# Gated conv + state-space trunk in float32: a new buffer layout, another load queue and fixed priorities in the combination stage

## The chip, the cores and the metric

The kernel runs on one core of one Trainium2 chip. The metric is the device time of one execution in microseconds (us); the median of three executions is given, with the lowest and the highest. Differences under about 0.3% of it can't be told from noise here.

A core has a matrix engine (PE, with its weight loads PEld), a vector engine (DVE), an activation engine (ACT) and GpSimd (POOL). SyncE (SP) only issues transfers. DVE, ACT, POOL and PE each work through their own instructions strictly in the order laid down when the kernel is built.

## The reference

One decoder layer over 1024 positions and 1024 channels, all float32:

```python
h = layer_norm(x, ln_in_g, ln_in_b)
u = h @ w_in                      # -> conv GLU, z, x/B/C, dt, gate_a, gate_b
v = a * sigmoid(g);  v = causal_dwconv(v, 31 taps)
y_a = silu(layer_norm(v)) @ w_conv_out
y   = ssd_chunked(x * dt, ...)    # state-space scan, 32 heads, 4 groups, chunks of 128
y_b = (rms_norm_per_group(y * silu(z)) * norm_w) @ w_ssm_out
mix = (sigmoid(gate_a) * y_a + sigmoid(gate_b) * y_b) @ w_o
h = layer_norm(alpha * h + mix)
h = layer_norm(alpha * h + conv_ffn(h))
```

The change touches how `y_a`'s layer norm, `y_b`'s group norm and the two gated sums are scheduled. What is computed stays the same.

## The kernel before

**Tiling.** Positions are worked in two halves of 512 (`hh` 0 and 1). Channels lie on the 128 partitions, positions along the free axis. Every float32 product is made of three products of rounded parts (`mm3`, lines 170 to 172): a *column* of 128 output channels over 1024 inputs is 24 matmuls of 128x512 (`project`), and it fills one of four PSUM banks (`bank(1)`, tile `acc`). A column's weights are loaded by SP (line 145), rounded on ACT (line 147), and their remainder made on DVE (line 151).

**Order.** A planner lays out each engine's instructions at build time: it runs a model of the machine and gives each engine the ready instruction that stands first. Where an instruction stands is its place in the program; `tc.high_priority(offset=n)` puts it n places earlier, with a negative n later. The places inside such a block don't count for what follows. On the chip every engine then keeps to that order, whatever is ready.

**Mixers** (`mixers`, one call for each half). For each of four groups: two columns for B and C, four for X, four for z, four for the conv GLU; then `ssd_group`, four chunks of 128 positions. A chunk is a chain over PE (transposes 497 to 501, products 536, 539, 544), ACT (504, 511, 514) and DVE (531, 554, 562, 565, 566). While a group's chunks run, PE fills its time with the next group's columns. `conv4` takes an X column out of its bank (ACT 404, 406) into a tile of `x4`, which has two slots: group g+1 writes where group g-1 was.

After its four chunks a group is normalised: `scaled` sums squares over partitions by a product with ones (PE 573), then square root (ACT 581), reciprocal (DVE 582), a trip through DRAM to spread the row over partitions (POOL 584, 585), and four multiplications (DVE 588). `parts` then makes rounded part (ACT 601) and remainder (DVE 602) of the group; only then is its `x4` slot free. For group g, both stand in the program right ahead of `ssd_group` of group g+1. `conv31` is the 31-tap convolution: 60 DVE steps for each group's pair of tiles (line 453), set 1500 places back so that DVE does them when it has nothing else. The first six of its eight tiles are stored to DRAM (463); the last two stay in memory.

**Combination** (`combine`). Eight gate columns (`gate`, sigmoid on ACT 669) alternate with eight columns of the second half of the state-space output; each is added to a stored partial sum `yb` (SP 677) and multiplied by its gate (DVE 681, 682) into `mb0` to `mb7`. Then come the layer norm of the eight convolved tiles: six are loaded back (SP 692), POOL adds all eight (697, 699), PE averages over partitions (701, the *mean product*), DVE subtracts, ACT squares, POOL adds up (710), PE averages again (712), and the tiles are scaled, passed through silu and split into `sT`. This norm stands after the eight columns in the program and is set 900 places ahead. Eight columns over `sT` follow. In the first half the input norm of the second half is made at the end (`ln_in_second`).

**Memory.** The pool of `combine` lies on the bytes of the pool of `mixers`, tile by tile in the order in which tags are first used, and each tile waits on the chip for the users of the bytes beneath it alone. Before, the order is gate, yb, mb0 to mb7, the convolved pairs c0 to c2, stats, sq, sT, c3. So the gate tiles lie on `rstd` and `m` of the mixers, yb on `cbm` and `u`, the convolved pairs on `x4`, `stats` and `sq` on `zs`, `c3` on the last tiles, `rows` and `ya`.

Of the kernel before, what the change touches and what calls it, by code (L numbers as in the profile page):

```python
# [8 lines left out]
F32 = mybir.dt.float32  # L9
# [7 lines left out]
P = 128  # L17
# [38 lines left out]
def kernel(  # L56
# [212 lines left out]
    def ln_in_second(pl):  # L269
# [14 lines left out]
        return hT  # L284
# [188 lines left out]
    def ssd_group(pl, hh, g, xT, BT, CT, zs):  # L473
# [10 lines left out]
        for c in range(4):  # L484
# [81 lines left out]
            V.tensor_add(ssum[:, cs], sq[:, 0], sq[:, 1])  # L566

        def scaled():
            rstd = pl.tile([P, HALF], F32, tag="rstd", name=f"rstd{hh}_{g}")
            rows = pl.tile([P, P], F32, tag="rows", name=f"rows{hh}_{g}")  # L570
            pv = bank(0)
            for j in range(4):
                TE.matmul(
                    pv[j * HEADS : (j + 1) * HEADS, :P],
                    ones[:, :HEADS],
                    ssum[:, j * P : (j + 1) * P],
                    start=True,
                    stop=True,
                    tile_position=(0, j * HEADS),
                )  # L580
# [16 lines left out]
        def parts(yT):  # L597
            ks = slice((g % 2) * 4, (g % 2) * 4 + 4)
            hi, lo = yT[:, 0, ks], yT[:, 1, ks]
            for n in (slice(0, 2), slice(2, 4)):  # L600
                A.copy(hi[:, n], xT[:, n])
                V.tensor_tensor(
                    out=lo[:, n], in0=xT[:, n], in1=hi[:, n].bitcast(F32), op=ALU.subtract
                )

# [19 lines left out]
    def mixers(hh, hT):  # L625
        pre = first_columns(hh, hT, (CT_B, CT_C, CT_X))
        with pool(f"mixers{hh}") as pl:
            time_steps(pl, hh, pre[0])
            scaled = parts = None
            for g in range(GROUPS):  # L630
# [12 lines left out]
                if g in (1, 2):  # L643
                    parts(yT)
                split_2 = parts
                scaled, parts = ssd_group(pl, hh, g, xT, BT, CT, zs)
                if g == 3:
                    ssm_out_first(pl, hh, yT)
                    yT = big_tile(f"yT{hh}_2")
                    split_2(yT)  # L650
                    gate_first(pl, hh, hT, range(3))
                    scaled()
                    parts(yT)
# [5 lines left out]
    def combine(hh, hT, yT, accs):  # L659

        with pool(f"comb{hh}") as pl:
            mb, gbs = [], []

            def gate():
                j = len(gbs)
                pg = bank(1)
                project(pg, weights(wcol[CT_GB + j], f"gb{hh}_{j}"), hT)
                gb = pl.tile([P, HALF], F32, tag="gate", bufs=3, name=f"gb{hh}_{j}")
                A.activation(out=gb, in_=pg, func=AF.Sigmoid)
                gbs.append(gb)  # L670

            gate()
            for j in range(8):
                if j < 7:
                    gate()
                ya = pl.tile([P, HALF], F32, tag="yb", bufs=2, name=f"yb{hh}_{j}")
                SY.dma_start(ya, y_scr[hh][j])
                ps = bank(1)
                project(ps, weights(wssm[j, 1], f"sp{hh}_{j}"), yT)
                m = pl.tile([P, HALF], F32, tag=f"mb{j}", name=f"mb{hh}_{j}")  # L680
                V.tensor_add(m, ya, ps)
                V.tensor_mul(m, m, gbs[j])
                mb.append(m)
            with tc.high_priority(offset=900):
                cs = []
                for i in range(8):
                    if i in accs:
                        cs.append(accs[i])
                        continue
                    if i % 2 == 0:  # L690
                        pair = pl.tile([P, 2, HALF], F32, tag=f"c{i // 2}", name=f"cc{hh}_{i}")
                    SY.dma_start(pair[:, i % 2, :], c_scr[hh][i])
                    cs.append(pair[:, i % 2, :])
                stats = pl.tile([P, 2, HALF], F32, tag="stats", name=f"stats{hh}")
                squares = pl.tile([P, 2, HALF], F32, tag="sq", name=f"csq{hh}")
                mean = stats[:, 0, :]
                G.tensor_add(mean, cs[0], cs[1])
                for c in cs[2:]:
                    G.tensor_add(mean, mean, c)
                pm = bank(0)  # L700
                TE.matmul(pm, mean_w, mean, start=True, stop=True)
                var = stats[:, 1, :]
                for i, c in enumerate(cs):
                    V.tensor_tensor(out=c, in0=c, in1=pm, op=ALU.subtract)
                    if i == 0:
                        A.activation(out=var, in_=c, func=AF.Square)
                    else:
                        sq = squares[:, i % 2, :]
                        A.activation(out=sq, in_=c, func=AF.Square)
                        G.tensor_add(var, var, sq)  # L710
                pv = bank(0)
# [4 lines left out]
                for i, c in enumerate(cs):  # L716
# [8 lines left out]
                    split_to(sT, i, c)  # L725
            mixT = big_tile(f"mixT{hh}")
# [8 lines left out]
            return mixT, None if hh else ln_in_second(pl)  # L735
# [554 lines left out]
```

## Time and profile before

| | us |
|---|---|
| median of 3 executions (lowest, highest) | 1969.62 (1964.88, 1970.72) |
| the profiled execution, its own time | 1972.21 |
| its span, first to last instruction | 1970.1 |
| busy: DVE | 1600.7 (81%) |
| busy: ACT | 1083.8 (55%) |
| busy: POOL | 203.1 (10%) |

The profiled execution is 2.1 us longer than its span and 2.6 us above the median. PE's busy time is a union of overlapping matmuls, each shown with its full latency of 0.39 us although the next one starts 0.23 us after it; so a full PE is seen by the number of matmuls in a stretch, and a wait by its gap. The first half's mixers run to about 484 us and its combination to about 626 us; the second half's mixers run from about 660 to 1135 us and its combination to about 1267 us. The rest is the feed-forward part.

### The profile page before, as it was taken

How to read it: one execution, taken by the hardware profiler on the slowest of the kernel's cores; microseconds unless marked ns; L12 is line 12 of the kernel's file. 1: busy time of each engine (PE TensorE's matmuls, PEld its weight loads, DVE VectorE, ACT ScalarE, POOL GpSimd, SP SyncE). 2: the span in 40 equal slices, each digit the busy share in tenths (PEclk: the TensorE clock that was granted, in tenths of full speed). 3: DMA queues.
4: the chain of work that ended last, by engine and by line, in shares of the span. 5: the costliest groups of instructions: out<-in, count | busy, mean ns of one | idle time of the engine just before them, and what ended most of it. 6: DMA issues, size and time to landing. Idle time of an engine off the chain costs nothing.

```text
span 1970.1 us, 25840 instructions
## 1 busy us (share of the span) xinstructions
PE 1932.9 (98%) x9453; PEld 1575.2 (80%) x9453; DVE 1600.7 (81%) x2224; ACT 1083.8 (55%) x1617; POOL 203.1 (10%) x246
## 2 busy tenths in 40 slices
PE   9999999999899999999999999999999999999997
PEld 8888777777688788888778888888888888878886
DVE  7599999999786547898999655587788888879778
ACT  4676767653263265868775435365555555544432
POOL 0001010110310000110101040001000000121010
PEclk9999999999999999999999999999999999999999
DMA  7645455546455665555554644576455555588673
GB/s 270 221 171 198 161 206 177 166 162 202 157 187 176 215 221 182 190 184 198 178 178 148 213 162 129 169 255 227 160 166 183 175 185 184 179 293 297 201 230 125
DMA packets 128416, 378.36 MB, mean 192 GB/s; under 512 B 15104, under 2 KB 15648, under 8 KB 128288
## 3 DMA queue, kind: packets, MB, share of 16 engines
q1 hardware_dynamic: 109152, 321.63, 48.7%
q0 software_dynamic: 12800, 43.54, 6.4%
q10 hardware_dynamic: 6336, 11.54, 1.6%
q8 instruction: 74, 1.21, 0.3%
q14 instruction: 54, 0.44, 0.1%
HBM read 289.99 MB, written 86.65 MB: 191 GB/s over the span
## 4 chain that ended last, share of the span: by engine, by line
PE 71%; DVE 16%; issue 5%; DMA 5%; ACT 2%; POOL 1%; SPq 0%; DVEq 0%; ACTq 0%; POOLq 0%
PE acc L172 16%; PE acc L171 16%; PE acc L170 16%; PE sm L171 6%; PE sm L172 6%; PE sm L170 6%; DVE c L453 5%; DVE w_c L151 1%; DVE x L408 1%; DMA rstd<-nrm_scr 1%; PE sm L536 1%; DMA dr<-wdown 1%; PE sm L539 1%; DVE x L588 1%; DMA b_scr<-fo 1%
## 5 line engine op out<-in xcount | busy, mean ns | idle before, releaser
L170 PE MATMUL acc<-hT,w_c 128*128 128x512 f32 x1000 | 391.8, 392 | 0.5 <-ACT x L406 0.5
L171 PE MATMUL acc<-hT,w_c 128*128 128x512 f32 x1000 | 390.7, 391 | 0.0
L172 PE MATMUL acc<-hT,w_c 128*128 128x512 f32 x1000 | 390.1, 391 | 0.6 <-DVE w_c L151 0.5
L453 DVE SCALAR_TENSOR_TENSOR c<-v,pc,c 128x512 f32<-128x512 f32 x480 | 370.6, 798 | 7.3 <-ACT c L442 4.7
L170 PEld LDWEIGHTS acc<-hT,w_c 128*128 128x128 f32 x1000 | 187.8, 188 | 41.7 <-issue 1.9
L172 PEld LDWEIGHTS acc<-hT,w_c 128*128 128x128 f32 x1000 | 187.8, 188 | 41.2 <-DVE w_c L151 1.4
L171 PEld LDWEIGHTS acc<-hT,w_c 128*128 128x128 f32 x1000 | 187.8, 188 | 39.2 <-issue 1.1
L147 ACT CAST w_c<-st_c 128x1024 fp32r<-128x1024 f32 x128 | 133.8, 1045 | 108.5 <-PE acc L172 90.0
L515 POOL TENSOR_TENSOR ce<-ce,xbc 128x1024 f32<-128x1024 f32 x28 | 74.1, 2648 | 694.3 <-ACT ce L514 694.3
L1077 ACT CAST w_dn<-dr 128x1024 fp32r<-128x1024 f32 (+1 forms) x73 | 68.8, 944 | 87.5 <-DMA dr<-wdown 25.3
L504 ACT ACTIVATE m<-ab,acs 128x128 f32<-128x128 f32 x256 | 78.4, 390 | 48.2 <-PE sm L536 47.0
L170 PE MATMUL sm<-h1s,w_s 128*128 128x512 f32 x264 | 102.7, 389 | 0.0
L171 PE MATMUL sm<-h1s,w_s 128*128 128x512 f32 x264 | 102.7, 389 | 0.0
L172 PE MATMUL sm<-h1s,w_s 128*128 128x512 f32 x264 | 102.2, 389 | 0.0
L151 DVE TENSOR_TENSOR w_c<-st_c,w_c 128x1024 fp32r<-128x1024 f32 x64 | 79.1, 1239 | 22.3 <-ACT w_c L147 22.1
L1078 DVE TENSOR_TENSOR w_dn<-dr,w_dn 128x1024 fp32r<-128x1024 f32 (+1 forms) x73 | 78.7, 1089 | 5.3 <-ACT w_dn L1077 5.3
L408 DVE SCALAR_TENSOR_TENSOR x<-u,pc,x 128x512 f32<-128x512 f32 x96 | 76.7, 810 | 5.7 <-ACT x L406 5.7
L172 PE MATMUL acc<-h1b,w_ue 128*128 128x512 f32 x176 | 68.9, 395 | 1.5 <-DVE w_ue L151 1.5
L170 PE MATMUL acc<-h1b,w_ue 128*128 128x512 f32 x176 | 68.8, 391 | 0.0
L171 PE MATMUL acc<-h1b,w_ue 128*128 128x512 f32 x176 | 68.6, 390 | 0.0
L170 PE MATMUL sm<-h1b,w_s 128*128 128x512 f32 x176 | 68.5, 389 | 0.0
L171 PE MATMUL sm<-h1b,w_s 128*128 128x512 f32 x176 | 68.5, 389 | 0.0
(324 smaller groups left out, 4542.3 us busy)
## 6 DMA issues: line engine op xcount, KB each, us to landing
st_c<-wcol SPq DMA_DIRECT2D x128, 512.0 KB, 4.4
low_scr<-w_c SPq DMA_DIRECT2D x64, 512.0 KB, 2.9
w_c<-low_scr SPq DMA_DIRECT2D x64, 512.0 KB, 4.4
ab<-acs_scr SPq DMA_DIRECT2D x32, 512.0 KB, 4.1
dr<-wdown SPq DMA_DIRECT2D x55, 256.0 KB, 4.8
st_wo<-wo SPq DMA_DIRECT2D x24, 512.0 KB, 4.0
st_ue<-wup SPq DMA_DIRECT2D x22, 512.0 KB, 4.2
first_scr<-first ACTq DMA_DIRECT2D x44, 256.0 KB, 2.9
```

The lines of the kernel that those rows point to most:

```text
L147: A.copy(w[:, 0, :], st)
L151: V.tensor_tensor(out=w[:, 1, :], in0=st, in1=w[:, 0, :].bitcast(F32), op=ALU.subtract)
L170: TE.matmul(ps, wa(0), xa(0), start=start, stop=False, skip_group_check=more)
L171: TE.matmul(ps, wa(0), xa(1), start=False, stop=False, skip_group_check=more)
L172: TE.matmul(ps, wa(1), xa(0), start=False, stop=stop, skip_group_check=more)
L408: V.scalar_tensor_tensor(out=o, in0=u[:, k : k + HALF], scalar=pc[:, wc + k : wc + k + 1], in1=o, op0=ALU.mult, op1=ALU.add,)
L453: V.scalar_tensor_tensor(out=accs[i], in0=v[:, k : k + HALF], scalar=pc[:, wc + k : wc + k + 1], in1=accs[i], op0=ALU.mult, op1=ALU.add,)
L504: A.activation(out=m[:, h, :], in_=ab[:, h, :], func=AF.Relu, scale=-1.0, bias=acs[:, c, 8 * g + h : 8 * g + h + 1],)
L515: G.tensor_tensor(out=ce, in0=ce, in1=CT[:, cs].unsqueeze(1).to_broadcast([P, 8, P]), op=ALU.mult)
L536: TE.matmul(o, xs[:, h * HP : (h + 1) * HP], m[:, h, :], start=True, stop=first)
L1077: A.copy(w[:, 0, cs], src)
L1078: V.tensor_tensor(out=w[:, 1, cs], in0=src, in1=w[:, 0, cs].bitcast(F32), op=ALU.subtract)
```

## The change

`combine` gets its tiles in another order: sq, stats, gate, yb, mb0 to mb7, in the first half c3 (as `x1_3`, for `ln_in_second`), c0 to c2, sT. The norm is cut into three functions. `early_tiles` runs after the first `yb` load: it makes the tiles, loads the six stored convolved tiles from POOL's queue instead of SP's, 5000 places ahead, and adds up the eight tiles on POOL. `deviations` (mean product, differences, squares) stands after pass j = 2 of the loop in the first half and j = 1 in the second; `normed` (second product, scaling, `sT`) after j = 4 and j = 3. The block set 900 places ahead is gone.

In the mixers, the four products with ones of groups 0 to 2 (line 573) are set 300 places back, and the two pieces of `parts` of groups 0 and 1 move from ahead of the next group's chunks to behind its chunks 0 and 1.

```diff
-            xt = pl.tile([P, D], F32, tag=f"c{t}", name=f"x1_{t}")
+            xt = x3 if t == 3 else pl.tile([P, D], F32, tag=f"c{t}", name=f"x1_{t}")
...
             V.tensor_add(ssum[:, cs], sq[:, 0], sq[:, 1])
+            if c < len(between):
+                between[c]()
...
-            pv = bank(0)
-            for j in range(4):
-                TE.matmul(
+            with tc.high_priority(offset=-300 if g < 3 else 0):
+                pv = bank(0)
+                for j in range(4):
+                    TE.matmul(
...
+            return [lambda: part(slice(0, 2)), lambda: part(slice(2, 4))]
...
-                if g in (1, 2):
-                    parts(yT)
+                between = parts(yT) if g in (1, 2) else []
                 split_2 = parts
-                scaled, parts = ssd_group(pl, hh, g, xT, BT, CT, zs)
+                scaled, parts = ssd_group(pl, hh, g, xT, BT, CT, zs, between)
...
+            gbs = []
+            squares = pl.tile([P, 2, HALF], F32, tag="sq", name=f"csq{hh}")
+            stats = pl.tile([P, 2, HALF], F32, tag="stats", name=f"stats{hh}")
+            late, cs = [], []
+            mean, var = stats[:, 0, :], stats[:, 1, :]
+
+            def early_tiles():
+                mb = [pl.tile([P, HALF], F32, tag=f"mb{j}", name=f"mb{hh}_{j}") for j in range(8)]
+                late.extend(
+                    pl.tile([P, D], F32, tag="c3", name=f"x1_{t}") for t in (3,) if not hh
+                )
+                pairs = [
+                    pl.tile([P, 2, HALF], F32, tag=f"c{i}", name=f"cc{hh}_{i}") for i in range(3)
+                ]
+                with tc.high_priority(offset=5000):
+                    for i in range(6):
+                        G.dma_start(pairs[i // 2][:, i % 2, :], c_scr[hh][i])
+                        cs.append(pairs[i // 2][:, i % 2, :])
+                cs.extend(accs[i] for i in (6, 7))
                 G.tensor_add(mean, cs[0], cs[1])
                 for c in cs[2:]:
                     G.tensor_add(mean, mean, c)
+                return mb
...
+            gate()
+            mb = None
+            for j in range(8):
+                if j < 7:
+                    gate()
+                ya = pl.tile([P, HALF], F32, tag="yb", bufs=2, name=f"yb{hh}_{j}")
+                SY.dma_start(ya, y_scr[hh][j])
+                if mb is None:
+                    mb = early_tiles()
+                ps = bank(1)
+                project(ps, weights(wssm[j, 1], f"sp{hh}_{j}"), yT)
+                V.tensor_add(mb[j], ya, ps)
+                V.tensor_mul(mb[j], mb[j], gbs[j])
+                if j == 2 - hh:
+                    deviations()
+                if j == 4 - hh:
+                    sT = normed()
```

More of the change, by code (lines that the diff above doesn't have):

```diff
@@ L471, in z_gate, with ssd_group @@
         return zs
-    def ssd_group(pl, hh, g, xT, BT, CT, zs):
+    def ssd_group(pl, hh, g, xT, BT, CT, zs, between):
         S = states[g]
@@ L599, in parts, with part @@
             hi, lo = yT[:, 0, ks], yT[:, 1, ks]
-            for n in (slice(0, 2), slice(2, 4)):
+            def part(n):
                 A.copy(hi[:, n], xT[:, n])
@@ L649, in mixers @@
                     yT = big_tile(f"yT{hh}_2")
-                    split_2(yT)
+                    for part in split_2(yT):
+                        part()
                     gate_first(pl, hh, hT, range(3))
                     scaled()
-                    parts(yT)
+                    for part in parts(yT):
+                        part()
                 with tc.high_priority(offset=-1500):
@@ L661, in combine @@
         with pool(f"comb{hh}") as pl:
[L662 to L696, printed above, removed]
+            gbs = []
@@ L734, in combine @@
                 split_to(mixT, j, mb[j])
-            return mixT, None if hh else ln_in_second(pl)
+            return mixT, None if hh else ln_in_second(pl, late[0])
     def out_proj(pl, rs, hh, mixT):
```

27 lines of the change are left out of this document (18 added, 9 removed).

## The prediction

> **What bounds the kernel now.** First the page, for the engine that sets the end.
>
> ```profile
> span 1970.1 us, 25840 instructions
> PE 1932.9 (98%) x9453; PEld 1575.2 (80%) x9453; DVE 1600.7 (81%) x2224; ACT 1083.8 (55%) x1617; POOL 203.1 (10%) x246
> ```
>
> PE is filled nearly throughout, and the change adds and removes no product. So it can only give or take time in which PE stands still. Those gaps are named, with their causes, in the view of waits on PE (total us, times, longest):
>
> ```profile
> PE sm L536 <- DVE m L531: 6.5, 5, 1.5
> PE sm L701 <- POOL stats L699: 5.2, 1, 5.2
> ...
> PE sm L573 <- DVE ssum L566: 1.8, 2, 0.9
> ...
> PE acc L170 <- ACT gb L669: 1.6, 1, 1.6
> ...
> PE acc L170 <- ACT x L406: 0.5, 1, 0.5
> ```
>
> Three of these the change works on: the mean product (701), the products with ones (573), the first sigmoids (669). The largest group, 536 waiting for the vector engine, it doesn't name. The stretch table gives the price of the longest wait, by the count of matmuls that began or ran in 20 us:
>
> ```profile
> 500.00:520.00 20.00, 18.37 (x81) 14.91 (x80) 12.43 (x16) 5.69 (x7) 2.91 (x3) 1.00 0.53 180
> 520.00:540.00 20.00, 14.78 (x50) 11.01 (x50) 16.52 (x18) 5.73 (x9) 13.07 (x9) 0.83 0.37 124
> 540.00:560.00 20.00, 20.00 (x88) 16.20 (x87) 14.02 (x14) 11.91 (x15) 6.03 (x5) 1.00 0.35 118
> 1140.00:1160.00 20.00, 20.00 (x88) 16.19 (x88) 9.15 (x11) 6.44 (x9) 10.25 (x7) 1.00 0.61 209
> ```
>
> A full stretch holds 88, so a matmul takes 20/88 = 0.227 us and a column of 24 takes 5.45. From 520 to 540 there are 38 fewer: 8.6 us, of which the wait is 5.2 and the rest the granted clock of 0.83 that follows it (the mean product's own two passes cost some 0.4 more than two plain matmuls). I put **8.2 us** on the mean product's wait. The last row is the second half's combination: full, nothing to win.
>
> **Why the mean product waits.** Timelines of DVE, SP, POOL, PE and ACT:
>
> ```profile
> 506.80 1.57 ACT L669 ACTIVATE gb<-acc 128x512 f32<-128x512 f32 x3
> 511.15 1.53 DVE L453 SCALAR_TENSOR_TENSOR c<-v,pc,c 128x512 f32<-128x512 f32 x2
> 511.63 2.98 SPq L692 DMA_DIRECT2D cc<-c_scr  x6
> 520.75 1.41 DVE L681 TENSOR_TENSOR mb<-yb,acc 128x512 f32<-128x512 f32 x2 [8.07 <-DMA yb<-y_scr]
> 516.76 1.28 POOL L697 TENSOR_TENSOR stats<-cc 128x512 f32<-128x512 f32 x1 [22.01 <-DMA cc<-c_scr]
> 518.29 5.71 POOL L699 TENSOR_TENSOR stats<-stats,cc 128x512 f32<-128x512 f32 x4 [0.25 <-DMA cc<-c_scr]
> 524.08 3.79 POOL L699 TENSOR_TENSOR stats<-stats,c 128x512 f32<-128x512 f32 x2
> 522.32 0.39 PE L172 MATMUL acc<-yT,w_sp 128*128 128x512 f32 x1
> 527.92 2.08 PE L701 MATMUL sm<-stats,mean_w 128*128 128x512 f32 x2 [5.22 <-POOL stats L699]
> ```
>
> The six stored tiles are asked for only at 511.6; five additions follow, then the two tiles kept in memory, which the convolution finished at 511.15 + 1.53 = 512.7. POOL has stood idle for 22 us before. With the six loaded early, on a queue with nothing else to do, only the last two additions follow 512.7.
>
> **The change, part by part.**
>
> *Loads on POOL.* Six issues leave SP (2.98 us), which also sends the yb loads 3 us sooner, and go to POOL, which is 10% busy; the bytes beneath (zs) were last read by the fourth group's chunks, ahead of all the columns from which `combine` starts. Cost on the path: none. Queued behind them on POOL are the group norm's trip through DRAM (584, 585), if the planner puts them first, and the additions; the trip would then wait for the stores of the third group's convolved tiles. I take nothing for it, since POOL was idle for 22 us after that trip.
>
> The Trainium skill ("DMA: Bandwidth & Descriptors", Latency and other measured facts) gives about 1 us to the first byte from GpSimd against 0.6 us from SP: an estimate by that page is 6 x 0.4 = 2.4 us against the change if the loads were late. No row here shows the first byte; the cover of tens of us hides it either way.
>
> *Additions on POOL, earlier.* They now lie beside the convolution, and there the two engines disturb each other:
>
> ```profile
> 428.83 1.40 DVE L453 SCALAR_TENSOR_TENSOR c<-v,pc,c 128x512 f32<-128x512 f32 x2
> 431.66 2.83 POOL L515 TENSOR_TENSOR ce<-ce,xbc 128x1024 f32<-128x1024 f32 x1 [12.29 <-ACT ce L514]
> 432.15 3.54 DVE L453 SCALAR_TENSOR_TENSOR c<-v,pc,c 128x512 f32<-128x512 f32 x2
> ```
>
> Two convolution steps take 1.40 alone and 3.54 beside 2.83 us of POOL: 0.76 us lost for each us of POOL. Five additions of 1.28 cost DVE 4.9 us. The early yb loads put three passes of 681 and 682 (0.7 each step by the row of 520.75, 1.4 a pass) ahead of the convolution, 4.2 us. So the last two tiles come at 512.7 + 4.9 + 4.2 = 521.8, less the idle time of DVE that is filled (bounded by 0 and the 9 us); with two additions, 2.6, the sum is ready between 515 and 524.
>
> *The fixed place.* Behind pass 2, PE has six matmuls more to do than at 522.3, less the 1.8 and 1.6 us of waits that go before it: it arrives at about 520.5 to 522. Against "ready" that leaves a wait of 0 to 4 us; I take **0.5**, as the filled idle time (8.07 us ahead of the first 681 alone) is nearer to all of the loss than to none. Saved: 8.2 - 0.5. Its second product (712) comes four columns, 21.8 us, later; the chain between them is eight differences and squares and seven additions at the 1.43 to 1.9 us of the rows above (5.71/4, 3.79/2), 10 to 13 us, so it stays hidden; without that cover, what exceeds 21.8 us would be PE's wait.
>
> *Sigmoids.* Gate tiles move off `rstd`, which the mixers give up last, onto `u` and `xbc`. The three sigmoids at 506.80 stand in a row, the first for a column that was done long before; banks then run out and PE waits 1.6 us. Whether the planner then puts them earlier, the trace can't say: 0 to 1.6, I take **0.8**.
>
> *Products with ones, 300 places back.* Both waits go: **1.8**. But what hangs behind them comes later too. Counted in the code, 300 places from there are what is left of `scaled` (8), four chunks and parts (about 200) and three columns of about 32: B, C and the first X of the next group. PE, at 98%, nearly always has something ready, so the products slip by some 20 us, and with them the release of the `x4` slot for which the X columns wait:
>
> ```profile
> L573 PE MATMUL sm<-ssum,ones x64: 272/285/297, 192.1 to 1107.5; 128*32 128x128 f32 x64
> ...
> 195.16 0.37 ACT L581 ACTIVATE rows<-sm,eps 128x128 f32<-128x128 f32 x1
> 198.28 0.95 DVE L582 RECIPROCAL rows<-rows 128x128 f32<-128x128 f32 x1
> 199.53 0.61 POOL L584 DMA_DIRECT2D nrm_scr<-rows  x1 [18.31 <-DVE rows L582]
> 203.53 0.58 POOL L585 DMA_DIRECT2D rstd<-nrm_scr  x1 [3.39 <-DMA nrm_scr<-rows]
> 209.37 2.74 DVE L588 SCALAR_TENSOR_TENSOR x<-x,pc,rstd 128x512 f32<-128x512 f32 x4 [3.98 <-DMA rstd<-nrm_scr]
> 212.14 1.05 ACT L601 CAST yT<-x 128x1024 fp32r<-128x1024 f32 x1 [0.27 <-DVE x L588]
> 219.50 2.35 DVE L602 TENSOR_TENSOR yT<-x,yT 128x1024 fp32r<-128x1024 f32 x2
> 222.00 1.27 ACT L406 ACTIVATE x<-acc,pc 128x512 f32<-128x512 f32 x2
> ...
> 228.37 0.44 PE L536 MATMUL sm<-m,xs 128*64 128x128 f32 x4
> ...
> 231.91 0.48 PE L171 MATMUL acc<-hT,w_c 128*128 128x512 f32 x1
> ```
>
> From the product at 192.1 to the X column's exit at 222.0 are 29.9 us. When the products come behind X0, the three other X columns (16.3) and a chunk's products (231.91 - 228.37 = 3.5) can still run, until the four banks are full: 19.9 us of cover. The same stretch stands four times, groups 0 and 1 of both halves. Without the waits between its pieces the chain takes 3.1 (to 195.16) + 0.37 + 0.95 + 4.0 + 5.84 + 2.74 + 1.05 + 2.35 + 0.69 = 21.1, which is 1.2 over the cover; with them 29.9, 10 over. Four times: 4.8 to 40 us. Below, 0, if the planner finds a hole in PE for the products earlier. I take the low end, **4.8**: DVE waits here are queueing behind convolution steps, and with the trip through DRAM (3.98 us of idle DVE), 588 and 602 gone from the stretch before, DVE should have caught up by the time they come. This choice decides most, and is the weakest.
>
> *Between the chunks.* `parts` behind chunks 0 and 1 lets chunk instructions go first; its own steps are the same. What PE waits for the chain, DVE uses: of the 6.5 us at 536 I take **2.4** off (half of 4.8).
>
> **Sum**: -8.2 + 0.5 - 0.8 - 1.8 + 4.8 - 2.4 = **-7.9 us**. Against the profiled execution's 1972.2 (span 1970.1 and 2.1 around it) that is 1964.3; against the median of 1969.6, 2.6 lower, **1961.7**. With the terms at their good ends (0 for the slot, 1.6 for the sigmoids) it is 1957, at their bad ones (4 us for the mean product) 1965.
>
> **Rivals.** *The slot costs what the other terms give.* With half of the queueing left, the chain is about 4 us over the cover in each place: 16, with 5 off at 536: -8.2 + 0.5 - 0.8 - 1.8 + 16 - 5 = +0.7, **1970**. For it: the first X column leaves its bank at 222.00, right as 602 ends (219.50 + 2.35), and at 968.32 the row below names 602 as what it waited for. Against: the one wait of PE named for it (406) is 0.5 us.
>
> *Slower: the slot's chain keeps its length.* The chain, from square root to exit, took much the same everywhere:
>
> ```profile
> 288.49 0.37 ACT L581 ACTIVATE rows<-sm,eps 128x128 f32<-128x128 f32 x1
> 314.63 1.27 ACT L406 ACTIVATE x<-acc,pc 128x512 f32<-128x512 f32 x2
> ...
> 849.05 0.37 ACT L581 ACTIVATE rows<-sm,eps 128x128 f32<-128x128 f32 x1
> 871.83 0.69 ACT L406 ACTIVATE x<-acc,pc 128x512 f32<-128x512 f32 x1
> ...
> 939.80 0.37 ACT L581 ACTIVATE rows<-sm,eps 128x128 f32<-128x128 f32 x1
> 968.32 0.69 ACT L406 ACTIVATE x<-acc,pc 128x512 f32<-128x512 f32 x1 [1.04 <-DVE yT L602]
> ```
>
> That is 26.8, 26.1, 22.8 and 28.5 us, plus 3 ahead: 9 over the cover, 36 in all. With all 6.5 at 536 won back: -10.3 + 36 - 6.5 = +19, **1989**. It decides from (5.9 + 10.3 + 6.5)/4 = 5.7 us over the cover. For it: order is fixed, and a step waits for its place even if its data is there. Against: PE's own waits in those places give DVE time to catch up, so the later chains shorten.
>
> *The change doesn't remove the wait.* DVE hands over the last two tiles late (POOL's additions, 681 and 682 ahead), PE waits some 5 us and loses the clock again: -7.9 + 5 = -2.9, **1967**. The Trainium skill ("GPSIMD Engine Reference", Key points) says that GpSimd shares its memory interfaces with the vector engine and contends with its instructions of two inputs in SBUF. The 3.54 against 1.40 us above agrees; by it the convolution, with two such inputs, always pays.
>
> **How the numbers follow.** About 0.3%, 5.9 us, is what a measurement tells from no change. Forecast (a gain of 6 to 14): 0.47. Slot gives back the gain: 0.24. Wait stays: 0.07. Slot's full chain: 0.22. So faster 0.47, same 0.31, slower 0.22. The range reaches from 1951 (all 6.5 at 536 gone too) to 1979, about half of the slow case.
>
> **What would show it.** Right: no wait at 701, 88 matmuls and clock 1.00 in every stretch of the first combination; POOL's loads and five additions done well before the convolution ends; 573 behind the first X column, and no column waiting on 406. Wrong: PE waiting for ACT 406 in the groups' second third, four times; 536 waiting longer; or 701 still idle for POOL. If 573 doesn't move, the slot's terms fall away.

## The result and the profile after

| | before | after |
|---|---|---|
| median of 4 executions (us) | 1967.38 | 1997.23 |
| lowest, highest | 1964.88, 1970.72 | 1995.01, 1998.48 |
| ratio, 95% interval | | 1.0149 (1.0128 to 1.0171) |
| the profiled execution (us) | 1972.21 | 1995.01 |
| its span (us) | 1970.1 | 1993.3 |

The change makes the kernel slower by 1.5%, 29.9 us between the medians and 23.2 us between the two profiled spans. The forecast was 1961.7 with a range up to 1979. The first lines of the page after:

```profile
span 1993.3 us, 25854 instructions
...
PE 1944.1 (98%) x9453; PEld 1580.7 (79%) x9453; DVE 1598.4 (80%) x2224; ACT 1085.7 (54%) x1617; POOL 210.8 (11%) x258
```

PE has as many instructions as before and is as "busy"; this line doesn't show where 23 us went. The view of PE's waits after does; its first line (total us, times, longest):

```profile
PE acc L170 <- ACT x L406: 26.8, 4, 10.5
```

The four causes shown of before (536, the mean product, 573, the sigmoids) are all gone from this list. In their place stands one that was 0.5 us: PE waits four times for ACT line 406, which takes X columns out of their banks. The stage borders tell the rest. These rows give, for the kernel before, the first start of the gate columns (the combination begins), of the output product (it ends), and of the second half's gate columns:

```profile
L170 PE MATMUL acc<-hT,w_gb x64: 389/389/632, 483.0 to 571.5; 128*128 128x512 f32 x64
...
L170 PE MATMUL acc<-w_wo,mixT x64: 389/389/476, 628.3 to 673.0; 128*128 128x512 f32 x64
...
L170 PE MATMUL acc<-hT,w_gb x64: 389/389/793, 1135.1 to 1212.3; 128*128 128x512 f32 x64
```

and for the kernel after:

```profile
L170 PE MATMUL acc<-hT,w_gb x64: 389/389/793, 503.7 to 580.9; 128*128 128x512 f32 x64
...
L170 PE MATMUL acc<-w_wo,mixT x64: 389/389/476, 637.7 to 682.4; 128*128 128x512 f32 x64
...
L170 PE MATMUL acc<-hT,w_gb x64: 389/389/793, 1158.2 to 1235.4; 128*128 128x512 f32 x64
```

The first half's mixers take 20.7 us more (503.7 against 483.0), its combination 11.3 less (134.0 against 145.3), the second half's mixers 13.7 more (520.5 against 506.8). That adds up to 23.1 of the 23.2 us. The combination gained more than the forecast, and the mixers lost three times as much (34.4 us). The stretch table after, for the two waits of the first half and for the stretch that held the mean product's wait before:

```profile
220.00:240.00 20.00, 14.18 (x68) 10.79 (x67) 19.52 (x30) 12.68 (x24) 0.58 (x1) 0.86 0.53 174
...
320.00:340.00 20.00, 11.38 (x63) 8.60 (x61) 17.80 (x29) 11.47 (x22) 1.17 (x2) 0.84 0.52 166
...
520.00:540.00 20.00, 20.00 (x90) 16.57 (x89) 9.74 (x8) 5.21 (x6) 7.61 (x5) 1.00 0.47 156
```

PE is idle for 6 and 9 us of two stretches, while DVE is busy for 19.5 and 17.8 of their 20. At 520 to 540 PE is now full.

How the first of the four waits comes about is read from the timelines of PE, ACT, DVE and POOL after:

```profile
209.16 0.41 PE L576 MATMUL sm<-ssum,ones 128*32 128x128 f32 x2
209.50 0.66 PE L497 MATMUL sm<-ident,x 128*128 128x128 f32 x4
...
211.76 0.49 PE L172 MATMUL acc<-hT,w_c 128*128 128x512 f32 x1
212.18 0.41 PE L576 MATMUL sm<-ssum,ones 128*32 128x128 f32 x2
212.52 0.50 PE L170 MATMUL acc<-hT,w_c 128*128 128x512 f32 x1
...
212.62 0.37 ACT L584 ACTIVATE rows<-sm,eps 128x128 f32<-128x128 f32 x1 [0.17 <-PE sm L576]
...
216.94 0.95 DVE L585 RECIPROCAL rows<-rows 128x128 f32<-128x128 f32 x1
...
218.19 0.61 POOL L587 DMA_DIRECT2D nrm_scr<-rows  x1 [35.94 <-DVE rows L585]
...
223.86 1.41 DVE L591 SCALAR_TENSOR_TENSOR x<-x,pc,rstd 128x512 f32<-128x512 f32 x2 [0.48 <-DMA rstd<-nrm_scr]
...
226.33 1.41 DVE L591 SCALAR_TENSOR_TENSOR x<-x,pc,rstd 128x512 f32<-128x512 f32 x2
...
230.61 1.22 DVE L606 TENSOR_TENSOR yT<-x,yT 128x1024 fp32r<-128x1024 f32 x1
231.74 0.69 DVE L521 TENSOR_TENSOR xs<-sm,dtv 128x512 f32<-128x512 f32 x1
...
234.45 1.23 DVE L606 TENSOR_TENSOR yT<-x,yT 128x1024 fp32r<-128x1024 f32 x1
...
235.72 1.84 ACT L406 ACTIVATE x<-acc,pc 128x512 f32<-128x512 f32 x3 [2.19 <-DVE yT L606]
236.46 0.79 PE L170 MATMUL acc<-hT,w_c 128*128 128x512 f32 x1 [5.82 <-ACT x L406]
```

The products with ones start at 209.16 instead of 192.15, behind the next group's first X column. From there to the exit of that column at 235.72 are 26.6 us. The exit is three columns at once (x3): they stood finished in their banks, since the `x4` slot was still in use, and when the fourth bank was full PE stopped for 5.82 us. Line 606 (602 before), the last user of the slot, was done at 234.45 + 1.23 = 235.68.

### The profile page after: what moved, and what is told of

Read it like the earlier page. It is cut to its first block, busy times and chain, and to the rows that moved or that the text cites. A ratio compares the mean times of both kernels' runs of the same rounds, so it can differ in the third digit from the quotient of the medians.

```text
span 1993.3 us, 25854 instructions
## 1 busy us (share of the span) xinstructions
PE 1944.1 (98%) x9453; PEld 1580.7 (79%) x9453; DVE 1598.4 (80%) x2224; ACT 1085.7 (54%) x1617; POOL 210.8 (11%) x258
## 4 chain that ended last, share of the span: by engine, by line
PE 42%; DVE 4%; DMA 3%; issue 1%; ACT 1%; SPq 0%; DVEq 0%; ACTq 0%
PE acc L172 8%; PE acc L171 8%; PE acc L170 8%; PE sm L171 6%; PE sm L172 6%; PE sm L170 6%; DMA dr<-wdown 1%; DMA t_scr<-fo 1%; DVE rows L231 1%; DVE w_dn L1100 0%; DVE rows L234 0%; DMA st_wo<-wo 0%; DMA first_scr<-first 0%; PE sm L536 0%; DVE fo L981 0%
## 5 line engine op out<-in xcount | busy, mean ns | idle before, releaser
L170 PE MATMUL acc<-hT,w_c 128*128 128x512 f32 x1000 | 395.4, 395 | 27.3 <-ACT x L406 26.8
L453 DVE SCALAR_TENSOR_TENSOR c<-v,pc,c 128x512 f32<-128x512 f32 x480 | 360.8, 784 | 10.2 <-ACT c L442 7.9
L170 PEld LDWEIGHTS acc<-hT,w_c 128*128 128x128 f32 x1000 | 189.7, 190 | 71.4 <-ACT x L406 28.5
L172 PEld LDWEIGHTS acc<-hT,w_c 128*128 128x128 f32 x1000 | 189.6, 190 | 40.7 <-issue 1.7
L171 PEld LDWEIGHTS acc<-hT,w_c 128*128 128x128 f32 x1000 | 189.8, 190 | 40.3 <-issue 1.8
```

Of the source, the lines that this page charges most:

```text
L170: TE.matmul(ps, wa(0), xa(0), start=start, stop=False, skip_group_check=more)
L171: TE.matmul(ps, wa(0), xa(1), start=False, stop=False, skip_group_check=more)
L172: TE.matmul(ps, wa(1), xa(0), start=False, stop=stop, skip_group_check=more)
L453: V.scalar_tensor_tensor(out=accs[i], in0=v[:, k : k + HALF], scalar=pc[:, wc + k : wc + k + 1], in1=accs[i], op0=ALU.mult, op1=ALU.add,)
```

## The experiments

Kernels that stand together below ran on one chip beside the kernel before; each ratio is against those runs.

### Which part costs: the change in four pieces

The first kernel keeps the mixers of before and has the whole new `combine`; the second adds the rounded parts behind the chunks, the third instead the late products; the fourth has the changed mixers and the old `combine`. Against the kernel after:

```diff
 e1, e2:
-            with tc.high_priority(offset=-300 if g < 3 else 0):
-                pv = bank(0)
+            pv = bank(0)
...
 e1, e3:
-                between = parts(yT) if g in (1, 2) else []
+                if g in (1, 2):
+                    for part in parts(yT):
+                        part()
+                between = []
 e4: combine() and ln_in_second() of before
```

> The combination's part of the change alone (new layout, loads on GpSimd, fixed places); the mixers as before. If the loss sits in the mixers, this gives what the traces of before and after show for the combination: the mean product's wait and the clock behind it, 8.2 us, and the sigmoids' wait, 1.6, both gone: about 1967.4 - 9.8 = 1957.6, between 1954 and 1961, no wait of the mean product on GpSimd, and the wait of X columns on ACT 406 at 0.5 us as before. If the combination's part takes time elsewhere (its rival), it is above 1964.

> The combination's part, and the rounded parts behind chunks 0 and 1, but the products with ones at their old place. Theory 'late products' (the 300 places delay the group norm's chain and with it the x4 slot): nothing waits for ACT 406 for more than 2 us in all, the time is within 3 us of the combination's part alone, about 1958. Rival 'remainder behind the chunk's work' (line 606 queues behind chunk 1's DVE steps and that holds the slot): four waits on 406 of 5 us and more stay, and the time is near 1985 to 1997.

> The combination's part, and the products with ones 300 places back, but the rounded parts ahead of the chunks as before. Theory 'late products': the chain starts 20 us late here too, so the four waits on ACT 406 stay, 20 to 27 us in all, and the time is 1990 to 1997. Rival 'remainder behind the chunk's work': the second remainder comes 3 to 6 us earlier in each place, the waits fall to under 8 us in all, and the time is 1957 to 1968.

> The mixers' part alone (late products and rounded parts behind the chunks); the combination as before. If the parts add up, it is the kernel after plus what the combination gains: 1997.2 + 9.8 = 2007, between 2002 and 2012, with the waits on ACT 406 near 27 us and the mean product's wait of 5 us back. If the new layout or the GpSimd loads are what delays the mixers (rival), the waits on 406 are under 5 us and the time is near 1967.

| kernel | median us (before beside it 1971.40) | ratio, 95% interval | waits on ACT 406 |
|---|---|---|---|
| e1, combination only | 1963.66 | 0.9965 (0.9952 to 0.9977) | 0.5 |
| e2, and parts between the chunks | 1964.99 | 0.9966 (0.9956 to 0.9977) | 0.4 |
| e3, and late products | 1996.25 | 1.0132 (1.0117 to 1.0148) | 25.6 |
| e4, mixers only | 1995.62 | 1.0131 (1.0116 to 1.0145) | 25.2 |

The row of e3's waits:

```profile
PE acc L170 <- ACT x L406: 25.6, 4, 9.4
```

The late products alone make the whole loss (e3). The parts between the chunks make none (e2 beside e1): that rival falls, although the row at 231.74 shows the second remainder (606 at 234.45) queued behind chunk 1's work. DVE's timeline of e3, without that edit, has it at the same place:

```profile
234.26 1.21 DVE L606 TENSOR_TENSOR yT<-x,yT 128x1024 fp32r<-128x1024 f32 x1
```

So the edit moved nothing there.

e1 missed its expectation, 1954 to 1961, on the dear side: 7.7 us under the median of before beside it, and not 9.8. (The range was set with 1967.4 for before; 7.7 us under that would lie within it.) e4, expected at 2002 to 2012 with the mean product's wait of 5 us back, missed by more: the parts do not add up. With the new `combine` the changed mixers give 1.0149 (1.0128 to 1.0171), without it 1.0131 (1.0116 to 1.0145), so on top of these mixers it is worth nothing that can be measured. The stage rows of e4 say why:

```profile
L170 PE MATMUL acc<-hT,w_gb x64: 387/389/799, 500.8 to 579.1; 128*128 128x512 f32 x64
...
L170 PE MATMUL acc<-w_wo,mixT x64: 389/389/476, 635.8 to 680.5; 128*128 128x512 f32 x64
```

and DVE's timeline of e4, with its last convolution step:

```profile
494.15 0.74 DVE L453 SCALAR_TENSOR_TENSOR c<-v,pc,c 128x512 f32<-128x512 f32 x1
```

The old combination takes 135.0 us here instead of 145.3, as short as the new one after (134.0). The convolution was done at 494.9, ahead of the combination's start at 500.8, where before it ended at 512.7; with that the old order makes PE wait for the mean product only 0.7 us. So the changed mixers give 10.3 of the 11.3 us of the kernel after without the new layout, at the price of the 20.7 us that PE lost there. Whether that price has to be paid for it is asked below.

### Where e1's gain went

e1's own stage: 140.1 us (623.5 - 483.4), 5.2 under before and 6 over the kernel after. Its timelines of POOL and DVE:

```profile
474.31 3.23 POOL L687 DMA_DIRECT2D cc<-c_scr  x6
...
489.71 2.10 POOL L690 TENSOR_TENSOR stats<-cc 128x512 f32<-128x512 f32 x1
...
490.57 5.19 DVE L453 SCALAR_TENSOR_TENSOR c<-v,pc,c 128x512 f32<-128x512 f32 x3
491.89 7.25 POOL L692 TENSOR_TENSOR stats<-stats,cc 128x512 f32<-128x512 f32 x4
...
519.05 1.53 DVE L453 SCALAR_TENSOR_TENSOR c<-v,pc,c 128x512 f32<-128x512 f32 x2
```

The loads went out 37 us earlier than before (474.31 against 511.63), and the five additions ran beside the convolution. Three convolution steps then took 5.19 us, 1.73 each, where two alone took 1.40 in before. The convolution ended at 520.6, 7.9 us later than the 512.7 of before; the prediction had 521.8 as its bad end. In f4 (below), the same kernel with additions that start only at 516.21, it ended at 511.01 + 1.53 = 512.5, which points to the early additions. No wait of the mean product is listed for e1, but the weight remainders in DVE's order come late, and PE waits for `w_gb` instead (0.6 us in before):

```profile
PE acc L172 <- DVE w_gb L151: 2.4, 2, 2.0
...
PE acc L170 <- ACT gb L730: 1.6, 1, 1.6
```

The Trainium skill ("GPSIMD Engine Reference", Specifications) says that GpSimd contends for memory interfaces with vector instructions of two SBUF inputs; these rows agree: a step is 2.5 times as long here.

### Whether it is the slot: the dose, and the slot set free

Two kernels set the products 230 and 260 places back, which puts them behind one and two of the next group's columns. In the third the products are as late as after, but the norm and the parts of groups 0 and 1 no longer hold the slot: they work on the group's tile of silu(z), so f3 leaves the norm of these two groups out and shows only what the slot costs.

```diff
 f1: offset=-230     f2: offset=-260     f3:
+        xN = zs if g < 2 else xT
...
-                    out=xT[:, i, :],
-                    in0=xT[:, i, :],
+                    out=xN[:, i, :],
+                    in0=xN[:, i, :],
...
-                A.copy(hi[:, n], xT[:, n])
+                A.copy(hi[:, n], xN[:, n])
```

(The subtraction that makes the remainder reads `xN` in f3 too.)

> The changed kernel with the products with ones set 230 places back instead of 300, which puts them behind one column (B) of the next group instead of behind four. Slot theory: in before the first X column leaves its bank at 222.0 us, while the four banks are full only at 230.2, so the chain has 8 us of slack; one column, 5.5 us, uses less than that, so the waits on ACT 406 are under 3 us in all, and the time is within 4 us of the products at their old place, 1961 to 1969. Rival: any delay past the next group's first column costs the same (products taken apart, chunk 0 held up): waits or lost PE time of 10 us or more, 1975 and above.

> The same with 260 places: behind two columns (B and C), 11 us late. Slot theory: 3 us over the slack at most in each of the four places, less what the chain shortens as the vector engine catches up: waits on ACT 406 of 0 to 10 us in all, time 1963 to 1978, between the kernel with 230 places and the one with 300. Rival (any delay costs the same): 1990 to 1997.

> The changed kernel, with the group norm's multiplications and the rounded parts of groups 0 and 1 working on the group's tile of silu(z) in place of its x4 tile; so the norm of the scan's output is left out for these groups, with as many instructions of the same shapes on each engine. The x4 slot is then free when the fourth chunk ends; the tile of silu(z) is needed again only four columns, 22 us, later. Slot theory: the waits on ACT 406 fall from 27 us to under 2, and the time falls by 25 to 35 us, to 1962 to 1972, although the products are as late as in the changed kernel. Rival (late products hurt by holding up the next group's chunk 0, or by being spread through a column): the time stays above 1985.

| kernel | median us (before beside it 1970.26) | ratio, 95% interval | waits on ACT 406 |
|---|---|---|---|
| f1, 230 places | 1970.21 | 1.0001 (0.9988 to 1.0014) | none listed |
| f2, 260 places | 1969.81 | 0.9993 (0.9979 to 1.0006) | 9.7 |
| f3, 300 places, slot free | 1965.25 | 0.9972 (0.9958 to 0.9985) | none listed |

f2's row in the waits, and f3's products with ones:

```profile
PE acc L170 <- ACT x L406: 9.7, 4, 5.4
```

```profile
209.53 0.41 PE L578 MATMUL sm<-ssum,ones 128*32 128x128 f32 x2
```

f3 decides about the loss. Its products come at 209.53, as late and as spread out as after, and the whole loss is gone, with no wait on 406: it is the slot, not the lateness, nor the spreading of the products, nor the later chunk 0. The chain didn't shorten in it: its second remainder starts at 240.18 in DVE's timeline, 5.7 us later than after, and nothing waits for it. The waits follow the dose: none with one column, 9.7 us with two, 25.6 to 26.8 with three (209.16 - 192.15 = 17.0 us are three columns of 5.45; "four" in the expectation of f1 is one too many). The times of f1 and f2 don't: their intervals overlap.

f1 is 1.2 us over its range, which was set with 1967.4 for before, while that took 1970.26 here. Nothing waits for the slot in it, so the rival "any delay costs the same" (1975 and above) doesn't hold either. Its trace has two waits at 536 of 2.3 and 2.1 us in the second half's mixers, the second followed by a slower clock (last section). Whether its loss against e2, 0.35%, comes from these was not tried and stays open.

f3 and f2 show something more: what the late products may be good for. DVE's busy time (third figure) of the first half's mixers, 100 to 483 us, in before and in f3:

```profile
100.00:483.00 383.00, 378.70 (x2025) 303.57 (x2024) 372.10 (x556) 248.30 (x425) 35.29 (x19) 1.00 0.53 182
```

```profile
100.00:483.00 383.00, 383.00 (x2034) 306.34 (x2033) 379.88 (x568) 250.12 (x427) 33.60 (x17) 1.00 0.54 184
```

DVE is idle for 3.1 us instead of 10.9, and PE (first figure) is full instead of 4.3 short. By the stage borders, the combination of f3 takes 135.9 us (617.5 - 481.6) and that of f2 134.0 (617.3 - 483.3), with mixers as long as before (483.0). So the short combination needs no such loss in the mixers. It goes with a convolution that is further on: of the kernels with the new `combine`, it ends at 507.4 in f2, at 506.56 + 3.47 = 510.0 in f3 and at 520.6 in e1, and the combination takes 134.0, 135.9 and 140.1 us. That the convolution makes it short, and nothing else that the late products move, is argued; it was not tried by itself. What f2 gains in the first half it gives back in the second (514.2 against 506.8), where its longest wait stands. That led to the last kernel, 260 places in the first half alone:

```diff
-            with tc.high_priority(offset=-300 if g < 3 else 0):
+            with tc.high_priority(offset=-260 if g < 3 and not hh else 0):
```

> The changed kernel with the products with ones 260 places back in the first half only, and at their old place in the second. With 260 in both halves the first half's mixers took as long as before (483.3 against 483.0 us), although X columns waited some 4 us for the slot there, and the convolution ended at 507.4 instead of 512.7 in before, so that the combination took 134.0 us instead of 145.3. Theory 'later products fill the vector engine': the gain comes without the second half's 5.4 us wait; first part to the end of the combination 617 us, the rest as with the old products (1963.3 - 622.1 = 1341.2), a span of 1958 to 1961 and a ratio of 0.993 to 0.996. Rival 'only waiting of PE in the mixers pays for the short combination': what the combination gains the mixers lose, and the ratio is 0.9965 or more, no better than the combination's part alone.

Measured: 1963.15 us beside 1970.85 for before, a ratio of 0.9955 (0.9938 to 0.9972). The ratio is in the theory's range, but its interval reaches into the rival's (0.9965 or more) and doesn't tell it from e1's 0.9965; the profiled span, 1961.7, is 0.7 us over the range. Its stage row for the combination's end:

```profile
L170 PE MATMUL acc<-w_wo,mixT x64: 389/389/476, 619.1 to 663.8; 128*128 128x512 f32 x64
```

The combination ends at 619.1, not at the 617 of the theory. That is 4.4 us ahead of e1 and 9.2 ahead of before, but the kernel is only level with e1 in the profiled span (1961.7 and 1961.6). By its ratio it is the best of all kernels run; that it beats e1 isn't shown.

### What carries the combination's gain

Four more kernels take the new `combine` apart, all with the mixers of before (f4 ran beside f1 to f3, and g1 to g3 beside each other):

```diff
 f4 (e1 with the loads on SyncE):
-                        G.dma_start(pairs[i // 2][:, i % 2, :], c_scr[hh][i])
+                        SY.dma_start(pairs[i // 2][:, i % 2, :], c_scr[hh][i])
 g1 (e1 with the norm in its old place):
-                if j == 2 - hh:
-                    deviations()
-                if j == 4 - hh:
-                    sT = normed()
+            with tc.high_priority(offset=900):
+                deviations()
+                sT = normed()
 g2 (before, with the loads moved alone):
-                    SY.dma_start(pair[:, i % 2, :], c_scr[hh][i])
+                    with tc.high_priority(offset=5000):
+                        G.dma_start(pair[:, i % 2, :], c_scr[hh][i])
 g3 (e1 with the yb loads on GpSimd too):
-                SY.dma_start(ya, y_scr[hh][j])
+                G.dma_start(ya, y_scr[hh][j])
```

> The combination's part alone, with the six loads of stored convolved tiles on SyncE's queue instead of GpSimd's, still 5000 places ahead. Theory 'place, not queue': what counts is that they are asked for early; 1962 to 1966, as the combination's part alone. Rival 'the queue matters': the loads wait in SyncE's order for the memory beneath them and hold up weight loads, or come late again; the mean product waits for GpSimd or weight casts wait for transfers by 3 us or more, 1967 to 1973.

> The combination's part alone, but the differences and the rest of the norm stand where they stood before: behind the eight columns, 900 places ahead. Theory 'the queue carries the gain': with the loads early on GpSimd the sum is ready at about 522 us, where the old place is too, so it costs 0 to 3 us against the fixed places: 1963 to 1967 beside 1970 for before. Rival 'the fixed place carries it': the mean product is again put ahead of a sum that isn't ready, GpSimd's last addition holds PE for 3 to 5 us, and the time is within 0.15% of before.

> Before, with nothing but the six loads moved to GpSimd's queue, 5000 places ahead; layout and places as before. The convolved pairs then lie on the x4 tiles, whose last user is the remainder of the fourth group at 485 to 489 us, so the loads can go out at 489 at the earliest, still 22 us before SyncE sent them. Theory 'the queue carries the gain': the mean product's wait of 5.2 us falls under 1.5, and the time falls by 4 to 8 us against before. Rival 'the layout carries it': the loads in GpSimd's order hold up its additions or the spreading of the group norm; the mean product waits 3 us or more, and no gain over 2 us is seen.

> The combination's part alone, with the loads of the stored partial sums (yb) on GpSimd's queue too. In the combination's part alone DVE waits 2.9 us for the first of them, which SyncE sends only at 519.6 us behind weight loads that wait for their buffers, and PE waits 1.8 us at 509 us as banks are held by columns that wait for it. If that is the cause, the 1.8 us and the vector engine's wait go, the first addition of a pass starts before 505 us, and the time is 1 to 4 us under the combination's part alone, 0.9945 to 0.996 of before. Rival: the additions then stand ahead of the convolution on the vector engine and its end comes later; PE waits at the mean product instead, and the ratio is 0.9965 or more.

| kernel | median us (before beside it) | ratio, 95% interval |
|---|---|---|
| f4, loads on SyncE | 1969.04 (1970.26) | 0.9994 (0.9982 to 1.0006) |
| g1, norm in its old place | 1966.52 (1970.64) | 0.9977 (0.9967 to 0.9987) |
| g2, loads on GpSimd alone | 1964.98 (1970.64) | 0.9969 (0.9958 to 0.9980) |
| g3, yb loads on GpSimd too | 1964.50 (1970.64) | 0.9965 (0.9952 to 0.9978) |

SyncE's timeline and PE's wait in f4:

```profile
511.12 0.33 SPq L145 DMA_DIRECT2D st_gb<-wcol  x1
511.50 2.98 SPq L687 DMA_DIRECT2D cc<-c_scr  x6
```

```profile
PE sm L697 <- POOL stats L692: 3.6, 1, 3.6
```

With layout and fixed places as in e1, but the loads on SyncE, they go out at 511.50, as in before (511.63), although they stand 5000 places ahead: in that queue's order they come behind a weight load. The mean product waits again, and the gain is gone. g2 is the counterpart, POOL's timeline of it:

```profile
485.39 3.23 POOL L693 DMA_DIRECT2D cc<-c_scr  x6 [14.04 <-DVE yT L602]
```

In the old layout the loads wait for the slot's last user, the remainder (602), and go out at 485.39 (the expectation had 489 as the earliest); that is early enough, no wait of the mean product is listed, and the ratio, 0.9969, can't be told from e1's. So an early place on a queue that gets to it carries the gain; the other queue without the early place was not run. The layout lets the loads go 11 us sooner, which buys nothing that these intervals show; nor do the fixed places, by g1's interval beside e1's. The shortest version that gains is g2: before, with six loads on another queue.

g3 followed neither its theory nor its rival. Its ratio is the rival's, but the additions don't stand ahead of the convolution and no wait of the mean product is listed. DVE's timeline has the first addition of a pass:

```profile
513.70 0.68 DVE L744 TENSOR_TENSOR mb<-yb,acc 128x512 f32<-128x512 f32 x1
```

The partial sum is there, and the addition still stands at 513.70, not before 505: its place in DVE's order is behind the convolution. PE's wait for the sigmoids stays at 1.6 us. In POOL's order a yb load now stands between the additions: it goes out at 514.69, after 24.57 us of waiting for DVE to free its buffer, and all but one of the additions come behind it.

## Why the prediction was wrong

- **The slot, +4.8 us, "this choice decides most, and is the weakest".** This is the step that failed. The start was right: 300 places put the products behind the first X column, and the named sign, PE waiting for 406 four times in the groups' second third, is what the profile shows. Cover was even a little longer than the 19.9 us of the text: PE's last matmul before the first wait starts at 236.46 - 5.82 - 0.39 = 230.25, 21.1 us after the first product. The chain was mis-sized: 26.6 us, where the low end had 21.1. The argument for that end, "DVE should have caught up by the time they come", falls on the rows above. The reciprocal starts 4 us after its square root's end (212.99), and the two remainders start 2.9 and 6.7 us after the last multiplication's (227.74). DVE was idle for 0.5 us of the stretch 220 to 240. What did get shorter is the trip through DRAM, from the store's issue to the first multiplication: 223.86 - 218.19 = 5.7 us instead of 209.37 - 199.53 = 9.8. All the rest of the chain, where the queueing is, took 20.9 us; in before it took 20.0, and the low end had 21.1 - 9.8 = 11.3. Row 209.50 names a reason that the prediction didn't see: chunk 0's transposes still follow right behind the first product, as they did before, so chunk 0's vector work moved with the chain. That it alone kept the queueing long wasn't tried. Chunk 1's stands in the chain after (231.74), but it did so before too, ahead of the remainders at 219.50:

```profile
216.78 0.68 DVE L521 TENSOR_TENSOR xs<-sm,dtv 128x512 f32<-128x512 f32 x1
```

- **A price left out.** In the mean product's wait the prediction counted the slower clock behind it; in the slot's it didn't. PE's timeline behind the second wait after:

```profile
341.86 0.80 PE L170 MATMUL acc<-hT,w_c 128*128 128x512 f32 x1 [10.48 <-ACT x L406]
...
347.13 0.39 PE L170 MATMUL acc<-hT,w_c 128*128 128x512 f32 x1
```

  Twelve matmuls take 347.13 - 341.86 = 5.3 us instead of 12 x 0.227 = 2.7: 2.5 us more, on top of 10.5. Counted the same way, 11, 8 and 7 slow matmuls behind the other three waits cost 2.4, 1.7 and 1.5 us. So the slot's term is 26.8 + 8.1 = 34.9 us where the sum had 4.8, and the mixers lost 34.4 by the stage borders; the rest nearly cancels (the spread products below, 10.1 us at most, against 8.3 saved at 536 and 573). The Trainium skill ("TensorE: Matmul & The Clock Gate", What's actually happening) has the array at half its clock after an idle window of about 3.4 us, and at full again after as long a busy one. The rate agrees: 0.43 us a matmul against 0.227. The lengths don't quite: the four slow stretches last 3.1 to 5.3 us, and in f1 a wait of 2.06 us was followed by one (last section).
- **The products with ones, -1.8.** Both waits are gone, but taken apart they cost PE more: at 211.76 to 212.52 one of them between two plain matmuls makes a step of 0.76 us, 0.53 over 0.227. PE's timeline of before has them together:

```profile
191.83 0.39 PE L172 MATMUL acc<-hT,w_c 128*128 128x512 f32 x1
192.15 0.43 PE L573 MATMUL sm<-ssum,ones 128*32 128x128 f32 x8
192.50 0.66 PE L497 MATMUL sm<-ident,x 128*128 128x128 f32 x4
```

  From the plain matmul's start to the transposes' there are 0.67 us, so the four cost 0.44, 0.11 each. At 0.42 more for each, the four products of groups 0 to 2 in both halves, 24 in all, are 10.1 us at most. That wasn't foreseen. f3 has the same spread and is faster than before all the same, so it doesn't make the loss; what f3 would gain without it was not tried.
- **The slower rival, 1989, "the chain keeps its length".** It named the mechanism and its four places. Its 9 us over the cover in each place was too much (26.8 in four, by the waits), its missing clock and spread products too little; that it had +19 against 23.2 between the spans is partly luck, since these errors offset each other. Its chance was 0.22, and the range reached only half of it.
- **The mean product, -8.2 + 0.5.** The wait is gone after, as forecast, but not by the named signs. In the kernel after, the loads go out at 505.34, behind the group norm's trip in POOL's order, and the additions run from 517.07 to 527.9, all of them behind the convolution's end (494.7). The mean product stands at 541.77, 38 us into the combination, as forecast (520.5 to 522 is 37.5 to 39 us behind 483.0), so it finds the sum ready. And e4 shows that the late products remove all but 0.7 us of it without the new `combine`; by itself that change gives 5.2 us in this stage (e1), since POOL's additions delay the convolution, a loss that the prediction had computed and thought to be filled by idle time.
- **The good end.** With 0 for the slot and 1.6 for the sigmoids the terms give 1961.7 - 4.8 - 0.8 = 1956, not the 1957 of the text; nothing hangs on it.
- **The yb loads.** They were to come 3 us sooner with the six loads gone from SyncE's queue. In SyncE's timeline of e1 they go out at 519.62, 4.9 us later than the 514.72 of before. The step was wrong. In g3, where they go out early, nothing shows as gained (0.9965 beside e1's 0.9965), though there they also held up POOL's additions.
- **Sigmoids, -0.8, and 536, -2.4.** After, both waits are gone whole (1.6 and 6.5). In e1 the sigmoids' 1.6 stays, and f3 has it too, so it isn't the gate tiles' new place that removes it. The reason named for 536, "What PE waits for the chain, DVE uses", isn't needed for it: in f3 PE doesn't wait for the chain, and 536 is at 0.4. What the late products did there, by moving chunk 0, is argued and wasn't tried by itself.

## What to carry to other kernels

Before an instruction is moved back, follow what hangs behind it to the buffer that it releases, and compare that chain, with every queue in it at its measured length, with the time until the buffer is wanted; here the slack was gone between one column and two. Where an engine's order is fixed, don't count on less queueing because a chain starts later: work that it queued behind can move with it, as chunk 0's did here. And test the parts of a change apart as well as together: here most of one part's gain in the combination was had by the other part as well.

## What was not expected of the hardware

The slower clock came after a wait that was much shorter than those above. PE's timeline of f1:

```profile
1005.19 0.44 PE L536 MATMUL sm<-m,xs 128*64 128x128 f32 x4 [2.06 <-DVE m L531]
...
1006.09 0.59 PE L536 MATMUL sm<-m,xs 128*64 128x128 f32 x4
...
1008.49 0.63 PE L171 MATMUL acc<-hT,w_c 128*128 128x512 f32 x1
```

After 2.06 us without work, from 0.9 us later on, matmuls take 0.63 us instead of 0.39. The other wait of f1 at 536 was longer, 2.30 us, and the stretch behind it keeps the full clock (the figure of 1.00):

```profile
969.13 0.44 PE L536 MATMUL sm<-m,xs 128*64 128x128 f32 x4 [2.30 <-DVE m L531]
```

```profile
970.00:980.00 10.00, 10.00 (x62) 8.07 (x58) 10.00 (x19) 8.39 (x14) 3.73 (x1) 1.00 0.59 210
```

So the length of a wait alone doesn't tell here whether the clock falls, and a slower clock can follow a wait of 2 us already. That the wait caused it is argued from the order in time; it was not tried.
